# A decoder layer with 32 experts: a pool opened ahead of the output projection holds five more tiles, the operand of the dispatch comes in two tiles, and two orders of instructions change

## The chip, the cores and the metric

One core of a Trainium2 chip runs the whole kernel. The metric is device time in microseconds of one execution. In this text PE is TensorE, DVE is VectorE, ACT is ScalarE, POOL is GpSimd, and SP is the queue that issues the weight transfers; SBUF is the on-chip memory of 128 partitions, PSUM the accumulators of TensorE in banks of 512 float32 columns.

## The reference

One layer on 272 rows (256 tokens and 16 meta tokens), width 2048, all in float32. A mixer of two branches ends in an output projection; then comes a mixture of 32 experts, of which each token uses two:

```python
def mixer(x, ...):
    ...
    merged = (jax.nn.sigmoid(gm) * (y_m @ w_pm)
              + jax.nn.sigmoid(ga) * (y_a.reshape(B, L, A_W) @ w_pa))
    return merged @ w_out

def hier_moe(x2, w_group, b_group, w_router, b_router, w_gate_up, w_down):
    ...                                  # group, then two experts in it, per token
    def run_block(args):
        toks, ws, e = args
        xb = x2[toks]
        gu = xb @ w_gate_up[e]           # 2048 x 1024
        hb = jax.nn.silu(gu[:, :D_FF]) * gu[:, D_FF:]
        return ((hb @ w_down[e]) * ws[:, None]).astype(x2.dtype)   # 512 x 2048
    ...

h = layer_norm(ALPHA * h + mix, ln1_g, ln1_b)
h = layer_norm(ALPHA * h + hier_moe(h, ...), ln2_g, ln2_b)
```

The weights of the 32 experts are 32 x 12 MiB; they are read once.

## The kernel before

**Output projection.** `w_out` comes in 16 blocks of 1 MiB (`wo_r`, line 114, three buffers), four for each of four column blocks n. ACT and DVE split each block into a high and a low part, and PE multiplies with both (`wo_p`, line 285). Meanwhile PE also turns the residual `u` column by column into `uTb` and multiplies it with the router's weights (`plg`).

**Weight stream.** The expert weights come in chunks of 1 MiB. In this text "chunk e,k" is the k-th of the eight gate/up chunks of expert e (`weg`), each 256 of the 2048 rows; a down-projection chunk is `wed`, and the last two experts' down projection comes in pieces by columns (`wel`). The dictionary `specs` sets one order for all of them; `issue(n)` puts the next ones, up to n in all, into SP's queue in that order. Each takes the next buffer from the list `free`; `used` gives the buffer back when PE has multiplied with the chunk. The list holds four buffers `x0` to `x3`, four `y0` to `y3`, four `m0` to `m3` and later `u0`, `u1`, each 8 KiB a partition, whose former contents die at different times: `m` with the last column block of the output projection, `u` in the first dispatch. The chunks in `extra` have buffers of their own that take no later chunk: 0,7 lies in four pieces in the tiles of `yh` and `yl`, and 1,0 and 1,1 lie in the place of the accumulator `acc`. The scheduler decides where the transfers stand between others on SP.

**Dispatch.** For each four experts, `dispatch(q)` gathers their tokens' rows by matmuls with a 0/1 matrix `oh`: 8 banks of PSUM, each with two halves of 256 columns (k even, k odd), and in each half two matmuls with the high part `uh` of the rows and two with the low part `ul`. DVE reads the even half into `xe` (line 1050), ACT the odd half (line 1047). The first dispatch does two banks ahead, and the other six one by one between the first gate/up chunks; the later ones do all eight together.

**Experts.** They go in pairs p: PE multiplies 16 gate/up chunks (`gu`), ACT and DVE make `hb`, PE turns it to `hT`; between the gate/up chunks of pair p it does the down projection of pair p-1 (`py`). ACT and DVE scale the result and split it (`yh`, `yl`, lines 1277 and 1278), PE scatters it back to token rows (`pc`), and DVE adds it to `acc` (line 1265). The last pair's down projection goes in five pieces of columns (`LASTP`, three of 512 and two of 256); for them `finish` also takes the statistics of the final normalisation on DVE (line 1250) and a product on POOL.

Of the kernel before, what the change touches and what calls it, by code (L numbers as in the profile page):

```python
# [12 lines left out]
F32 = mybir.dt.float32  # L13
F32R = mybir.dt.float32r
# [9 lines left out]
P = 128  # L24
D = 2048
KD = D // P
# [22 lines left out]
def trunk(ctx, tc, x, meta, ln_emb_g, ln_emb_b, rel_bias, w_in, conv_w, conv_b, b_ig, b_fg,  # L49
# [796 lines left out]
    def in_parts(nm, src):  # L846
        ws = [pre.tile([P, 512], F32, name=f"{nm}{i}", tag=("yh", "yl")[i % 2], bufs=2)
              for i in range(4)]
        for i, w in enumerate(ws):
            nc.sync.dma_start(out=w, in_=src[:, i // 2, i % 2 * 512:i % 2 * 512 + 512])  # L850
        return lambda kk, h: ws[2 * kk + h]

    extra.update({("g", 0, 7): in_parts, ("g", 1, 0): lambda *a: in_acc(0, *a),
# [10 lines left out]
    uTb = big.tile([P, 8, S], F32, name="uTb", tag=YT[3])  # L864
# [35 lines left out]
    for n in range(4):  # L900
        sl = slice(n * 512, n * 512 + 512)
        pts = tchunks(w_out, KD, mh_, ml_, n * 512, f"wo{n}")
        issue((4, 8, 10, 10)[n])
        for b in range(2):
            uv = u[b][:, sl]
            nc.vector.scalar_tensor_tensor(uv, uv, ALPHA, pts[b], op0=ALU.mult, op1=ALU.add)
            nc.vector.bn_stats(ust[:, b, n], uv)
        if n < 3:
            bg.append(route_cols(n))
        else:  # L910
            drain()
            for _ in route_cols(n):
                pass
# [5 lines left out]
    issue(NSLOT + 3)  # L919
# [97 lines left out]
    def dispatch(q):  # L1017
# [8 lines left out]
        xe = me.tile([P, KD, 4 * C], F32, name=f"xe{q}", tag="xe", bufs=1)  # L1026
        ohf = oh.rearrange("p b e c -> p b (e c)")

        def bank(kc):
# [10 lines left out]
            for k in (2 * kc, 2 * kc + 1):  # L1040
                pv = pt[:, k % 2 * 256:k % 2 * 256 + 256]
                for i, part in enumerate((uh, ul)):
                    for b in R2:
                        mm(pv, lhsT=part[:, b, rows_of(k)], rhs=ohf[:, b],
                           start=i == 0 and b == 0, stop=i == 1 and b == 1)
                if k % 2:
                    nc.scalar.activation(xe[:, k], pv, AF.Identity, bias=gbp[:, 1, k:k + 1],  # L1047
                                         scale=gbp[:, 0, k:k + 1])
                else:
                    nc.vector.tensor_scalar(xe[:, k], pv, gbp[:, 0, k:k + 1],  # L1050
                                            gbp[:, 1, k:k + 1], op0=ALU.mult, op1=ALU.add)
# [5 lines left out]
    def slots_of(q, ohf):  # L1057
# [9 lines left out]
        ohT = me.tile([P, 2, S], F32R, name=f"ohT{q}", tag="ohT", bufs=1)  # L1067
# [52 lines left out]
    def up_chunk(e, kc, xe, pg_):  # L1120
# [4 lines left out]
        for kk in range(2):  # L1125
            k = kc * 2 + kk
            lt = xe[:, k, s0:s0 + C]
            mm(pg_[other], lhsT=lt, rhs=w(kk, 0), start=k == 0,
                             stop=k == KD - 1)
            mm(pg_[mine], lhsT=lt, rhs=w(kk, 1), start=k == 0,  # L1130
                             stop=k == KD - 1)
# [7 lines left out]
    def up_turn(p, hb):  # L1139
# [4 lines left out]
        hT = me.tile([P, 4, P], F32, name=f"hT{p}", tag="hT", bufs=1)  # L1144
# [14 lines left out]
    issue(NSLOT + 5)  # L1159
# [78 lines left out]
    def rows_split():  # L1238
        nonlocal gr
        h = pre.tile([P, 512], F32R, name="grh", tag="yh", bufs=2)  # L1240
        gr = me.tile([P, 512], F32R, name="gr", bufs=1)
# [42 lines left out]
    for p in range(NE // 2):  # L1284
# [4 lines left out]
        for n in range(16):  # L1289
# [19 lines left out]
            if n == 7:  # L1309
                hb = me.tile([P, 512], F32, name=f"hb{p}", tag="hb", bufs=1)  # L1310
# [24 lines left out]
    f12 = me.tile([P, 2, D], F32, name="fin12", tag="xe", bufs=1)  # L1335
    fin += [f12[:, 0], f12[:, 1]]
    final_scale()
    nm5 = me.tile([P, 2, 4, 32], F32, name="nm5", tag="hb", bufs=1)
    nc.vector.memset(nm5, 1.0)
    gated = gated_of(LAST, cur)  # L1340
    for c0, n in LASTP:
# [5 lines left out]
        gated(c0, n, py)()  # L1347
# [101 lines left out]
    nmT = me.tile([P, 2, P], F32R, name="nmT", tag="hT", bufs=1)  # L1449
# [43 lines left out]
```

## Time and profile before

| | before |
|---|---|
| time, median of 3 runs (lowest, highest) | 1781.91 us (1778.19, 1784.15) |
| the profiled execution's own time, its span | 1773.8 us, 1772.1 us |
| busy share of the span: PE, DVE, ACT, POOL | 93%, 40%, 26%, 7% |
| mean granted TensorE clock | 0.98 of 2.4 GHz |
| read from HBM, written | 533.53 MB, 2.11 MB |
| weight chunks `weg`, `wed`, issue to landing (median) | 19.9 us |

The busy share is an average over stages with different limits, and a matmul's end is modelled, so 93% doesn't say that PE bounds the kernel; which resource is full is read stage by stage. The time that a weight chunk takes from issue to landing includes its place behind others that were issued before it.

### The profile page before, as it was taken

How to read it: one execution, taken by the hardware profiler on the slowest of the kernel's cores; microseconds unless marked ns; L12 is line 12 of the kernel's file. 1: busy time of each engine (PE TensorE's matmuls, PEld its weight loads, DVE VectorE, ACT ScalarE, POOL GpSimd, SP SyncE). 2: the span in 40 equal slices, each digit the busy share in tenths (PEclk: the TensorE clock that was granted, in tenths of full speed). 3: DMA queues.
4: the chain of work that ended last, by engine and by line, in shares of the span. 5: the costliest groups of instructions: out<-in, count | busy, mean ns of one | idle time of the engine just before them, and what ended most of it. 6: DMA issues, size and time to landing. Idle time of an engine off the chain costs nothing. (4 is left out here: it accounts for less than half of the span.)

```text
span 1772.1 us, 20945 instructions
## 1 busy us (share of the span) xinstructions
PE 1648.9 (93%) x8488; PEld 1013.8 (57%) x8488; DVE 707.9 (40%) x1178; ACT 457.5 (26%) x695; POOL 118.2 (7%) x143
## 2 busy tenths in 40 slices
PE   8999999999999999989989899899897988988986
PEld 7988899988787787873343433432433334324332
DVE  7666754454646556452223323421212123202224
ACT  5343444444443443341110100110111001101111
POOL 3002000000302102000100000000000000000002
PEclk9999999999999999999999999999999999999998
DMA  7534454456565578648999999999999999999993
GB/s 221 169 108 132 144 167 143 143 190 229 179 204 178 167 260 301 222 165 303 418 419 420 419 420 419 420 420 419 420 419 419 419 420 420 419 420 419 420 409 118
DMA packets 155941, 537.06 MB, mean 303 GB/s; under 512 B 15724, under 2 KB 64076, under 8 KB 107824
## 3 DMA queue, kind: packets, MB, share of 16 engines
q1 hardware_dynamic: 153552, 530.54, 77.8%
q0 software_dynamic: 2224, 5.12, 1.0%
q8 instruction: 68, 1.11, 0.3%
q14 instruction: 33, 0.27, 0.0%
q10 hardware_dynamic: 64, 0.02, 0.0%
HBM read 533.53 MB, written 2.11 MB: 302 GB/s over the span
## 5 line engine op out<-in xcount | busy, mean ns | idle before, releaser
L1007 PE MATMUL gu<-weg,xe 128*64 128x512 f32 x2032 | 495.5, 610 | 30.5 <-DMA weg<-in_w_gate_up_dram 30.4
L1007 PEld LDWEIGHTS gu<-weg,xe 128*64 128x64 f32 x2032 | 140.2, 139 | 312.0 <-issue 246.9
L1007 PE MATMUL py<-wed,hT 128*64 128x512 f32 x960 | 246.4, 597 | 0.0
L1007 PEld LDWEIGHTS py<-wed,hT 128*64 128x64 f32 x960 | 69.6, 139 | 140.1 <-issue 138.7
L1277 ACT ACTIVATE yh<-py,gsl 128x512 fp32r<-128x512 f32 (+1 forms) x65 | 44.2, 681 | 355.3 <-PE py L1007 340.7
L1278 DVE SCALAR_TENSOR_TENSOR yl<-py,gsl,yh 128x512 fp32r<-128x512 f32 (+1 forms) x65 | 48.0, 738 | 194.4 <-ACT yh L1277 194.4
L1137 DVE TENSOR_TENSOR hb<-gu,hb 64x512 f32<-64x512 f32 x32 | 22.0, 689 | 243.7 <-ACT hb L1136 243.6
L1265 DVE TENSOR_TENSOR acc<-pc,acc 128x512 f32<-128x512 f32 (+1 forms) x122 | 78.9, 678 | 88.1 <-PE pc L1007 87.3
L1136 ACT ACTIVATE hb<-gu 64x512 f32<-64x512 f32 x32 | 18.9, 591 | 341.6 <-PE gu L1007 341.6
L1007 PE MATMUL pxe<-oh,uh 128*128 128x256 f32 x256 | 61.1, 321 | 46.1 <-DVE xe L1050 42.7
L1007 PEld LDWEIGHTS pxe<-oh,uh 128*128 128x128 f32 x256 | 40.9, 199 | 67.8 <-DVE xe L1050 55.8
L1251 POOL TENSOR_TENSOR fin<-acc,fin 128x512 f32<-128x512 f32 (+1 forms) x10 | 10.3, 1053 | 895.0 <-DVE acc L1265 895.0
L1050 DVE TENSOR_SCALAR xe<-pxe,gbp 128x256 f32<-128x256 f32 x64 | 34.7, 543 | 83.8 <-PE pxe L1007 83.8
L1007 PE MATMUL pc<-yh,ohT 128*128 128x512 f32 (+1 forms) x130 | 59.8, 460 | 6.0 <-ACT yh L1277 3.5
L1047 ACT ACTIVATE xe<-pxe,gbp 128x256 f32<-128x256 f32 x64 | 36.0, 563 | 101.1 <-PE pxe L1007 101.1
L1007 PEld LDWEIGHTS pc<-yh,ohT 128*128 128x128 f32 x130 | 24.7, 190 | 54.9 <-issue 23.8
L1007 PE MATMUL pc<-yl,ohT 128*128 128x512 f32 (+1 forms) x130 | 52.4, 403 | 1.1 <-DVE yl L1278 0.9
L1007 PE MATMUL pxe<-oh,ul 128*128 128x256 f32 x256 | 52.4, 287 | 0.0
L1068 DVE TENSOR_SCALAR ohT<-prk,slot 128x512 fp32r<-128x512 f32 x8 | 6.0, 751 | 93.7 <-PE prk L1007 93.7
L1007 PEld LDWEIGHTS pxe<-oh,ul 128*128 128x128 f32 x256 | 41.4, 201 | 0.0
L1007 PEld LDWEIGHTS pc<-yl,ohT 128*128 128x128 f32 x130 | 25.0, 193 | 4.6 <-DVE yl L1278 2.5
L760 POOL TENSOR_TENSOR gms<-gms,gas 128x512 f32<-128x512 f32 x8 | 10.9, 1389 | 224.0 <-DVE gas L759 224.0
(924 smaller groups left out, 3036.7 us busy)
## 6 DMA issues: line engine op xcount, KB each, us to landing
weg<-in_w_gate_up_dram SPq DMA_DIRECT2D x253, 1024.0 KB, 19.9
wed<-in_w_down_dram SPq DMA_DIRECT2D x120, 1024.0 KB, 19.9
gm_r<-in_w_in_dram SPq DMA_DIRECT2D x16, 1024.0 KB, 5.0
ga_r<-in_w_in_dram SPq DMA_DIRECT2D x16, 1024.0 KB, 5.1
wo_r<-in_w_out_dram SPq DMA_DIRECT2D x16, 1024.0 KB, 5.4
qk_r<-in_w_in_dram SPq DMA_DIRECT2D x8, 1024.0 KB, 5.7
mv_r<-in_w_in_dram SPq DMA_DIRECT2D x8, 1024.0 KB, 5.3
aq_r<-in_w_in_dram SPq DMA_DIRECT2D x8, 1024.0 KB, 5.2
```

Of the source, the lines that this page charges most:

```text
L760: nc.gpsimd.tensor_tensor(sg[0][:, b], sg[0][:, b], sg[1][:, b], op=ALU.add)
L1007: late(nc.tensor.matmul(*a, **k))
L1047: nc.scalar.activation(xe[:, k], pv, AF.Identity, bias=gbp[:, 1, k:k + 1], scale=gbp[:, 0, k:k + 1])
L1050: nc.vector.tensor_scalar(xe[:, k], pv, gbp[:, 0, k:k + 1], gbp[:, 1, k:k + 1], op0=ALU.mult, op1=ALU.add)
L1068: nc.vector.tensor_scalar(ohT.rearrange("p a b -> p (a b)"), pr, slot, None, op0=ALU.is_equal)
L1136: nc.scalar.activation(hb[mine], pg_[other], AF.Silu)
L1137: nc.vector.tensor_tensor(hb[mine], pg_[mine], hb[mine], op=ALU.mult)
L1251: nc.gpsimd.tensor_tensor(fin[1 + b][:, c0:c0 + n], acc[:, b, c0:c0 + n], fin[0][:, c0:c0 + n], op=ALU.mult)
L1265: nc.vector.tensor_tensor(av, pc[:, :n], av, op=ALU.add)
L1277: nc.scalar.activation(yh[:, :n], py[:, :n], AF.Copy, scale=gate)
L1278: nc.vector.scalar_tensor_tensor(yl[:, :n], py[:, :n], gate, yh[:, :n].bitcast(F32), op0=ALU.mult, op1=ALU.subtract)
```

## The change

It has four parts.

- Chunk 0,6 comes in four pieces into the places of `hb`, `hT`, `gr` and `ohT`, and these four tiles and the tile `xa` move from the pool `me`, opened behind the output projection, to the pool `pre`, opened ahead of it. `uTb` leaves the buffer `y3` and shares `xa`.
- `issue` is called with 12 in place of 10 in the third and fourth column block, and with one more in the two calls behind; so 1,2 and 1,3 are issued under the output projection (into `y2`, `y3`), 1,4 to 1,7 into `m0` to `m3`, and the first two `wed` into `u0`, `u1`.
- `xe` becomes two tiles of eight k each (`xa` in `pre`, `xb` in `me`); in `bank`, the matmuls of both halves come first and both reads after them.
- In the loop over the last pieces, the combination of a piece is written behind the matmuls of the next piece.

```diff
-    def in_parts(nm, src):
-        ws = [pre.tile([P, 512], F32, name=f"{nm}{i}", tag=("yh", "yl")[i % 2], bufs=2)
-              for i in range(4)]
+    def in_parts(tags, nm, src):
+        ws = [pre.tile([P, 512], F32, name=f"{nm}{i}", tag=t, bufs=4 // len(tags))
+              for i, t in enumerate(tags * (4 // len(tags)))]
...
-    extra.update({("g", 0, 7): in_parts, ("g", 1, 0): lambda *a: in_acc(0, *a),
+    extra.update({("g", 0, 6): lambda *a: in_parts(("hb", "hT", "gr", "ohT"), *a),
+                  ("g", 0, 7): lambda *a: in_parts(("yh", "yl"), *a), ("g", 1, 0): lambda *a: in_acc(0, *a),
                   ("g", 1, 1): lambda *a: in_acc(1, *a)})
...
-    uTb = big.tile([P, 8, S], F32, name="uTb", tag=YT[3])
+    uTb = pre.tile([P, 8, S], F32, name="uTb", tag="xa")
...
     for n in range(4):
         sl = slice(n * 512, n * 512 + 512)
         pts = tchunks(w_out, KD, mh_, ml_, n * 512, f"wo{n}")
-        issue((4, 8, 10, 10)[n])
+        issue((4, 8, 12, 12)[n])
...
-    issue(NSLOT + 3)
+    issue(NSLOT + 4)
     free += [(up, t) for t in UT]
...
-        xe = me.tile([P, KD, 4 * C], F32, name=f"xe{q}", tag="xe", bufs=1)
+        xe = [pool.tile([P, 8, 4 * C], F32, name=f"xe{q}{i}", tag=("xa", "xb")[i], bufs=1)
+              for i, pool in enumerate((pre, me))]
...
                     for b in R2:
                         mm(pv, lhsT=part[:, b, rows_of(k)], rhs=ohf[:, b],
                            start=i == 0 and b == 0, stop=i == 1 and b == 1)
+            for k in (2 * kc, 2 * kc + 1):
+                pv = pt[:, k % 2 * 256:k % 2 * 256 + 256]
                 if k % 2:
-                    nc.scalar.activation(xe[:, k], pv, AF.Identity, bias=gbp[:, 1, k:k + 1],
+                    nc.scalar.activation(xe[k // 8][:, k % 8], pv, AF.Identity, bias=gbp[:, 1, k:k + 1],
                                          scale=gbp[:, 0, k:k + 1])
                 else:
-                    nc.vector.tensor_scalar(xe[:, k], pv, gbp[:, 0, k:k + 1],
+                    nc.vector.tensor_scalar(xe[k // 8][:, k % 8], pv, gbp[:, 0, k:k + 1],
                                             gbp[:, 1, k:k + 1], op0=ALU.mult, op1=ALU.add)
...
-        ohT = me.tile([P, 2, S], F32R, name=f"ohT{q}", tag="ohT", bufs=1)
+        ohT = pre.tile([P, 2, S], F32R, name=f"ohT{q}", tag="ohT", bufs=1)
...
-            lt = xe[:, k, s0:s0 + C]
+            lt = xe[k // 8][:, k % 8, s0:s0 + C]
...
-        hT = me.tile([P, 4, P], F32, name=f"hT{p}", tag="hT", bufs=1)
+        hT = pre.tile([P, 4, P], F32, name=f"hT{p}", tag="hT", bufs=1)
...
-    issue(NSLOT + 5)
+    issue(NSLOT + 6)
...
-        gr = me.tile([P, 512], F32R, name="gr", bufs=1)
+        gr = pre.tile([P, 512], F32R, name="gr", bufs=1)
...
-                hb = me.tile([P, 512], F32, name=f"hb{p}", tag="hb", bufs=1)
+                hb = pre.tile([P, 512], F32, name=f"hb{p}", tag="hb", bufs=1)
...
-    f12 = me.tile([P, 2, D], F32, name="fin12", tag="xe", bufs=1)
-    fin += [f12[:, 0], f12[:, 1]]
+    fin += [pool.tile([P, D], F32, name=f"fin{i + 1}", tag=("xa", "xb")[i], bufs=1)
+            for i, pool in enumerate((pre, me))]
     final_scale()
-    nm5 = me.tile([P, 2, 4, 32], F32, name="nm5", tag="hb", bufs=1)
+    nm5 = pre.tile([P, 2, 4, 32], F32, name="nm5", tag="hb", bufs=1)
...
     gated = gated_of(LAST, cur)
+    then = None
     for c0, n in LASTP:
         py = pyp.tile([P, 512], F32, name=f"py{LAST}_{c0}", tag="py")
         for kk in range(4):
             for i in range(2):
                 mm(py[i * 64:i * 64 + 64, :n], lhsT=hTs[LAST][:, kk, 64 - i * 64:128 - i * 64],
                                  rhs=live["l", NE - 2 + i, c0][:, kk], start=kk == 0, stop=kk == 3)
-        gated(c0, n, py)()
+        nxt = gated(c0, n, py)
+        if then:
+            then()
+        then = nxt
+    then()
```

Where this puts the instructions, at three places. First SP's queue at the first dispatch: the transfers that are issued as PE uses up the first chunks (`weg_3` is chunk k = 3 of its expert, here experts 1 and 2; `wed_0`, `wed_1` are chunks of the down projection). Before:

```order
L823 DMA wed_0_7052<-in_w_down_dram 128x2048
L823 DMA weg_0_7069<-in_w_gate_up_dram 128x2048
L823 DMA weg_1_7088<-in_w_gate_up_dram 128x2048
L823 DMA weg_2_7105<-in_w_gate_up_dram 128x2048
L823 DMA weg_7_7027<-in_w_gate_up_dram 128x2048
L823 DMA wed_0_7029<-in_w_down_dram 128x2048
L823 DMA weg_3_7124<-in_w_gate_up_dram 128x2048
L823 DMA wed_1_7141<-in_w_down_dram 128x2048
L823 DMA wed_1_7147<-in_w_down_dram 128x2048
L823 DMA weg_4_7169<-in_w_gate_up_dram 128x2048
```

and with the change:

```order
L823 DMA weg_0_7061<-in_w_gate_up_dram 128x2048
L823 DMA weg_1_7078<-in_w_gate_up_dram 128x2048
L823 DMA weg_2_7097<-in_w_gate_up_dram 128x2048
L823 DMA weg_3_7114<-in_w_gate_up_dram 128x2048
L823 DMA wed_0_7036<-in_w_down_dram 128x2048
L823 DMA wed_0_7038<-in_w_down_dram 128x2048
L823 DMA wed_1_7133<-in_w_down_dram 128x2048
L823 DMA wed_1_7150<-in_w_down_dram 128x2048
L823 DMA weg_4_7176<-in_w_gate_up_dram 128x2048
```

Chunk 1,7 (`weg_7`) stood fifth among them and now stands ahead of the dispatch; nine rows stood ahead of `weg_4` (chunk 2,4), and now eight do.

Then PE in the second dispatch, where the eight banks lie together (`pxe_0`, `pxe_1`, `pxe_2` are banks; a wait is for the engine in brackets). Before:

```order
L1007 MATMUL pxe_0_7470<-oh_7466,uh 128x256 [waits DVE_49]
L1007 MATMUL pxe_0_7470<-oh_7466,uh 128x256
L1007 MATMUL pxe_0_7470<-oh_7466,ul 128x256 x2
L1007 MATMUL pxe_0_7470<-oh_7466,uh 128x256 [waits DVE_49]
L1007 MATMUL pxe_0_7470<-oh_7466,uh 128x256
L1007 MATMUL pxe_0_7470<-oh_7466,ul 128x256 x2
L1007 MATMUL pxe_1_7481<-oh_7466,uh 128x256 x2
L1007 MATMUL pxe_1_7481<-oh_7466,ul 128x256 x2
L1007 MATMUL pxe_1_7481<-oh_7466,uh 128x256 [waits DVE_49]
L1007 MATMUL pxe_1_7481<-oh_7466,uh 128x256
L1007 MATMUL pxe_1_7481<-oh_7466,ul 128x256 x2
L1007 MATMUL pxe_2_7492<-oh_7466,uh 128x256 [waits Activation_49]
```

and with the change:

```order
L1008 MATMUL pxe_0_7478<-oh_7473,uh 128x256 [waits DVE_49]
L1008 MATMUL pxe_0_7478<-oh_7473,uh 128x256
L1008 MATMUL pxe_0_7478<-oh_7473,ul 128x256 x2
L1008 MATMUL pxe_0_7478<-oh_7473,uh 128x256 x2
L1008 MATMUL pxe_0_7478<-oh_7473,ul 128x256 x2
L1008 MATMUL pxe_1_7489<-oh_7473,uh 128x256 [waits DVE_49]
L1008 MATMUL pxe_1_7489<-oh_7473,uh 128x256
L1008 MATMUL pxe_1_7489<-oh_7473,ul 128x256 x2
L1008 MATMUL pxe_1_7489<-oh_7473,uh 128x256 x2
L1008 MATMUL pxe_1_7489<-oh_7473,ul 128x256 x2
L1008 MATMUL pxe_2_7500<-oh_7473,uh 128x256 [waits Activation_49]
```

The matmuls are the same and stand in the same order; the wait for DVE in the middle of each bank is gone, and a bank's first matmul waits for DVE or, from the third on, for ACT. In the first dispatch it is the same, there with `gu` rows between the banks.

Last PE at the first two of the five last pieces (`py_0`, `py_512` are the products of the pieces, `pc_00` and `pc_01` the two halves of the scatter of the first). Before:

```order
L1007 MATMUL py_0_11275<-wel_0_11117,hT_11229 64x512
L1007 MATMUL pc_00_11288<-yh_0_11284,ohT_11142 128x512
L1007 MATMUL pc_00_11288<-yl_0_11285,ohT_11142 128x512
L1007 MATMUL pc_01_11295<-yh_0_11284,ohT_11142 128x512
L1007 MATMUL pc_01_11295<-yl_0_11285,ohT_11142 128x512
L1007 MATMUL py_512_11302<-wel_512_11119,hT_11229 64x512
L1007 MATMUL py_512_11302<-wel_512_11127,hT_11229 64x512
```

and with the change:

```order
L1008 MATMUL py_0_11290<-wel_0_11131,hT_11243 64x512
L1008 MATMUL py_512_11303<-wel_512_11133,hT_11243 64x512
L1008 MATMUL py_512_11303<-wel_512_11141,hT_11243 64x512
L1008 MATMUL py_512_11303<-wel_512_11133,hT_11243 64x512
L1008 MATMUL py_512_11303<-wel_512_11141,hT_11243 64x512
L1008 MATMUL py_512_11303<-wel_512_11133,hT_11243 64x512
L1008 MATMUL py_512_11303<-wel_512_11141,hT_11243 64x512
L1008 MATMUL py_512_11303<-wel_512_11133,hT_11243 64x512
L1008 MATMUL py_512_11303<-wel_512_11141,hT_11243 64x512
L1008 MATMUL pc_00_11316<-yh_0_11299,ohT_11156 128x512
L1008 MATMUL pc_00_11316<-yl_0_11300,ohT_11156 128x512
L1008 MATMUL pc_01_11323<-yh_0_11299,ohT_11156 128x512
```

The scatter of a piece moved behind all eight matmuls of the next piece; on DVE the statistics and the additions of one piece now stand between the scaling and the additions of the next.

## Rows read from the trace of the kernel before

**Rows 1.** The page, part 2: the span in 40 equal slices of 44.3 us; busy share of PE in tenths (9 is 90% or more), and GB/s that the DMA engines moved. The seventeenth to the twentieth digit and number are 709 to 886 us.

```profile
PE   8999999999999999989989899899897988988986
GB/s 221 169 108 132 144 167 143 143 190 229 179 204 178 167 260 301 222 165 303 418 419 420 419 420 419 420 420 419 420 419 419 419 420 420 419 420 419 420 409 118
```

**Rows 2.** Busy time of each engine in two stretches of 10 us around the first dispatch: stretch, its length, then busy us and instructions of PE, PEld, DVE, ACT, POOL; the last three columns are the granted TensorE clock as a share of full speed, the DMA engines' busy share, and GB/s.

```profile
790.00:800.00 10.00, 8.05 (x25) 4.61 (x26) 2.99 (x6) 7.01 (x15) 0.00 (x0) 0.52 0.00 0
830.00:840.00 10.00, 10.00 (x48) 3.19 (x46) 0.60 (x2) 0.59 (x1) 0.00 (x0) 1.00 0.87 322
```

**Rows 3.** Timeline of the SP queue from 799 to 836 us (start, time from the first issue to the last one's end, line, buffer and tensor, how many in a row).

```profile
799.95 0.33 SPq L823 DMA_DIRECT2D wed<-in_w_down_dram  x1
803.88 10.19 SPq L823 DMA_DIRECT2D weg<-in_w_gate_up_dram  x4
814.35 0.33 SPq L823 DMA_DIRECT2D wed<-in_w_down_dram  x1
815.71 0.33 SPq L823 DMA_DIRECT2D weg<-in_w_gate_up_dram  x1
819.66 4.27 SPq L823 DMA_DIRECT2D wed<-in_w_down_dram  x2
830.47 5.48 SPq L823 DMA_DIRECT2D weg<-in_w_gate_up_dram  x4
```

**Rows 4.** Timeline of PE from 790 to 839 us: start, us, operation, output and operands, how many, and in brackets the idle time before it and what ended it. `pxe` is the dispatch, `gu` the experts' gate/up product.

```profile
790.60 0.80 PE L1007 MATMUL pxe<-oh,uh 128*128 128x256 f32 x2 [1.19 <-ACT u L948]
792.54 0.80 PE L1007 MATMUL pxe<-oh,uh 128*128 128x256 f32 x2 [0.71 <-DVE xe L1050]
793.13 0.63 PE L1007 MATMUL pxe<-oh,ul 128*128 128x256 f32 x2
793.56 0.63 PE L1007 MATMUL pxe<-oh,uh 128*128 128x256 f32 x2
...
796.40 3.50 PE L1007 MATMUL gu<-weg,xe 128*64 128x512 f32 x8
799.84 0.52 PE L1007 MATMUL pxe<-oh,uh 128*128 128x256 f32 x2
800.19 0.40 PE L1007 MATMUL pxe<-oh,ul 128*128 128x256 f32 x2
801.23 0.51 PE L1007 MATMUL pxe<-oh,uh 128*128 128x256 f32 x2 [0.64 <-DVE xe L1050]
...
801.91 1.94 PE L1007 MATMUL gu<-weg,xe 128*64 128x512 f32 x8
803.77 0.52 PE L1007 MATMUL pxe<-oh,uh 128*128 128x256 f32 x2
...
828.54 10.47 PE L1007 MATMUL gu<-weg,xe 128*64 128x512 f32 x48
```

**Rows 5.** Timeline of PE, 1690 to 1720 us: the only two rows there that waited for a weight transfer.

```profile
1694.77 3.68 PE L1007 MATMUL gu<-weg,xe 128*64 128x512 f32 x8 [4.44 <-DMA weg<-in_w_gate_up_dram]
...
1709.73 1.94 PE L1007 MATMUL gu<-weg,xe 128*64 128x512 f32 x8 [0.51 <-DMA weg<-in_w_gate_up_dram]
```

**Rows 6.** Timeline rows of one `w_out` block: its issue on the SP queue, and the first instruction that reads it (ACT).

```profile
727.03 0.37 SPq L114 DMA_DIRECT2D wo_r<-in_w_out_dram  x1
...
738.77 1.05 ACT L122 CAST wo_20h<-wo_r 128x1024 fp32r<-128x1024 f32 x1 [1.48 <-PE wo_p L285]
```

**Rows 7.** The page, part 6: DMA issues of one kind: buffer and tensor, queue, how many, KB each, median us from issue to landing.

```profile
wo_r<-in_w_out_dram SPq DMA_DIRECT2D x16, 1024.0 KB, 5.4
```

**Rows 8.** Chain of waits of PE over the whole span: what waited, for what, us in total, how often, longest.

```profile
PE pxe L1007 <- DVE xe L1050: 42.7, 64, 1.0
```

**Rows 9.** Timeline rows of dispatches: the DVE and the ACT instruction that read the two halves of one bank of the first dispatch (800 us), then four PE rows from the middle of the third (1003 us).

```profile
800.63 0.54 DVE L1050 TENSOR_SCALAR xe<-pxe,gbp 128x256 f32<-128x256 f32 x1 [4.23 <-PE pxe L1007]
...
802.02 0.56 ACT L1047 ACTIVATE xe<-pxe,gbp 128x256 f32<-128x256 f32 x1 [2.86 <-PE pxe L1007]
...
1002.76 0.51 PE L1007 MATMUL pxe<-oh,uh 128*128 128x256 f32 x2 [0.91 <-DVE xe L1050]
...
1003.35 0.40 PE L1007 MATMUL pxe<-oh,uh 128*128 128x256 f32 x2
1003.59 0.40 PE L1007 MATMUL pxe<-oh,ul 128*128 128x256 f32 x2
1004.63 0.51 PE L1007 MATMUL pxe<-oh,uh 128*128 128x256 f32 x2 [0.64 <-DVE xe L1050]
```

**Rows 10.** Timeline of all engines from 1729 us on, rows of the first of the five last pieces, and the last DVE row before the final normalisation.

```profile
1729.90 3.65 PE L1007 MATMUL py<-wel,hT 128*64 128x512 f32 x16
...
1734.32 0.75 DVE L1278 SCALAR_TENSOR_TENSOR yl<-py,gsl,yh 128x512 fp32r<-128x512 f32 x1 [5.26 <-ACT yh L1277]
...
1734.34 0.49 PE L1007 MATMUL pc<-yh,ohT 128*128 128x512 f32 x1 [0.79 <-ACT yh L1277]
...
1735.66 1.29 DVE L1265 TENSOR_TENSOR acc<-pc,acc 128x512 f32<-128x512 f32 x2 [0.59 <-PE pc L1007]
...
1736.02 3.65 PE L1007 MATMUL py<-wel,hT 128*64 128x512 f32 x16
...
1736.87 1.40 DVE L1250 BATCH_NORM_STATS2 st<-acc 128x6 f32<-128x256 f32 x4
...
1756.02 0.74 DVE L1250 BATCH_NORM_STATS2 st<-acc 128x6 f32<-128x256 f32 x2
```

More of the change, by code (lines that the diff above doesn't have):

```diff
@@ L1448, in trunk @@
         nc.tensor.transpose(pn5[:, b], nm5[:, b].rearrange("p a b -> p (a b)"), ident)
-    nmT = me.tile([P, 2, P], F32R, name="nmT", tag="hT", bufs=1)
+    nmT = pre.tile([P, 2, P], F32R, name="nmT", tag="hT", bufs=1)
     nc.vector.tensor_copy(nmT, pn5)
```

## The prediction, made before the changed kernel had run

> **What bounds the kernel now.** I read the 40 slices first, to see which resource is full in which stretch. From the twentieth slice (842 us) to the third last, DMA moves 418 to 420 GB/s without a dip; the three from 709 to 842 us move 222, 165 and 303 [rows 1]. So the expert weights bound the second half, and the first half is bound by something else. Then the windows, for where the change-over lies: 790 to 800 us moves nothing, 830 to 840 us 322 GB/s [rows 2]. Then the SP queue, which issues the weights in its order, each when its buffer is free: nine chunks at 799.95 to 823.6 us, a pause, and from 830.47 us on four in 5.5 us [rows 3]. The pause is PE's doing: a chunk's buffer comes free when PE has multiplied it, and the three chunks after the seventh (0,7; 1,0; 1,1) lie in buffers that take no later chunk, so nothing is issued until chunk 1,2 has been used, in the stream that ends with 48 `gu` rows at 828.54 us [rows 4]. From there a chunk costs PE about 1.7 us (10.47 us for 48 rows of eight a chunk) against 1.05 MB / 420 GB/s = 2.5 us on the DMA engines, so the queue never empties again. Hence three stretches: PE's pace up to the 25th issue (830.47 us); then the DMA engines alone; and, after the last gate/up chunks (PE last waits for one at 1709.73 us [rows 5]), a chain of PE, ACT and DVE. What brings the 25th issue forward brings forward all weights after it by as much. A wait on PE in between is worth nothing.
>
> **More chunks under the output projection.** Sixteen chunks are now in SP's queue before the dispatch instead of fifteen, two of them between the `w_out` blocks. I cost this at nothing, for and against. For: the order on SP shows that the 25th chunk still waits for the use of 1,2. Before, 15 ahead and 9 until the pause make 24; after, 16 and 8 (0,6 now lies in pieces and frees no buffer) make 24 too. The DMA engines have emptied their queue by then, so a chunk loaded earlier only lengthens the pause. Against: the two chunks take 5.0 us of DMA in slices that move 165 to 222 GB/s. A `w_out` block is issued 11.7 us before its first use (727.03 to 738.77 us [rows 6]) and lands 5.4 us after its issue [rows 7]: 6.3 us of cover, 3.8 behind a chunk. If that cover were gone, each block would cost PE what it comes late. The pieces of 0,6 wait for what the pieces of 0,7 waited for before. The smaller tiles (`hb`, `hT`, `gr`, `ohT`) are written only after 0,6 has been used, and `uTb`'s place is read for the last time before `xe` needs it: nothing.
>
> **Halves of a bank.** In all 64 banks of the dispatches PE stops between the halves until DVE has read the first, 42.7 us in all [rows 8], most often 0.64 us, as at 801.23 [rows 4]. Only the first dispatch lies before the 25th issue, so only its eight banks count.
> Two banks ahead of the first `gu`, at the lower clock: now 790.60 to 796.40 = 5.80 us. Without a stop, sixteen matmuls go at the pace of the rows at 792.54, 793.13 and 793.56: one pair 0.59, seven 0.43, and 0.12 to switch: 3.72. That saves 2.1.
> Six banks between `gu` chunks, full clock: now 799.84 to 801.91 = 2.07 each. Without a stop: 0.35 (799.84 to 800.19), three pairs of 0.24 (1003.35 to 1003.59 [rows 9]), 0.09 to switch: 1.16. That saves 0.91 each, 5.5.
> The granted clock is 1.2 GHz from about 790 to 799.6 us (mean 0.52 [rows 2]; `gu` takes 3.50 at 796.40 and 1.94 at 801.91); before it fell PE had been idle, waiting for the routing, and before it rose it had run a `gu` chunk of 3.50 us without a stop. If it rises at the same moment, the third bank now falls into that stretch and takes 2.0 instead of 1.16: minus 0.8. If it rises sooner because PE now runs without stops from 790.60, that 0.8 is not lost, and the first `gu` (3.50 against 1.94 at full clock) gets up to 1.6 back. I take the same moment, the case the rows show: 2.1 + 5.5 - 0.8 = **6.8 us**; ends 6 (each bank 0.1 late for another reason) and 9 (the clock). The 25th issue comes at about 823.7 us. Are the 24 through by then? By the same savings the last five are issued from about 808 to 814 us and need 12.5 us: done about 822, just in time. That caps any further gain at some 2 us.
> The reads now both follow the second half. In the order after, ACT's read waits for DVE's, so a bank is free 0.54 + 0.56 us [rows 9] and three hand-overs of about 0.1 after its last matmul, 2.5 us after its first. In the first dispatch that is covered: a `gu` chunk of 1.9 us lies between banks, and two banks are used in turn. In the later ones two banks in turn give 1.25 us a bank against 1.87 now (1002.76 to 1004.63): 5 us less PE time a dispatch, under DMA, worth nothing.
> The Trainium skill ("PSUM — Partial Sum Buffer", PSUM bank collisions raise a hardware error) has a rule that speaks against this part: no two engines may access one bank at once, not even to read it, and waits go by the bank, not by the columns. The rows agree (PE waits for DVE though it writes other columns); two reads at once are shown by no row. By the rule a later bank costs 1.25 us, without it PE's own 1.07; the sum is the same by both.
>
> **The last pieces.** Now a piece of 512 columns takes 6.12 us (1729.90 to 1736.02): 3.45 of matmuls, then PE waits for `yh` and `yl`, then 1.2 for the four `pc` matmuls (1734.34 to 1736.02 less 0.46 of waiting for `yl`) [rows 10]. After, PE runs the next piece's `py` during `yh` and `yl`. I lay it out from the start of the first piece: `py` at 0, 3.45 and 8.2; `pc` of the pieces at 7.0, 11.7, 14.7. From the third on DVE is late: per piece it has 0.75 (`yl`), 1.29 (`acc`) and 1.40 (statistics) [rows 10], with about 2.0 for each piece of 256 columns 14.3 us over the five, in an order that mixes two pieces, and PE's second `pc` half waits for a bank that DVE reads late (15.4). Then `py` of the last piece 16.0 to 17.75, its `yl` 18.75 to 19.25, its `acc` to 22.15, its statistics to 22.9. Before, they end at 1756.02 + 0.74 - 1729.90 = 26.9. Gain **4.0 us**; ends 2 (each mixed DVE step 0.5 late) and 5.9 (PE alone). The weights are there: the last slice (from 1728 us) moves 118 GB/s, 5.2 MB [rows 1], 2.1 of them the output, so 3.1 MB of weights remain, 8 us at 2.5 us a chunk, through at about 6; the last are needed at 16.0.
>
> **Sum.** The profiled execution took 1773.8 us (span 1772.1): 1773.8 - 6.8 - 4.0 = 1763.0. The median of the runs shown, 1781.9, is 8.1 above it; the terms are differences, so I take them off the median too: **1771.1 us**, -0.6%. About 0.3% (5.3 us) is what a measurement can tell from no change.
>
> **Rivals.**
> (a) *A slow clock at the end.* Later dispatches are 5 us shorter, so PE reaches the DMA engines' pace earlier and stands longer at the two down-projection chunks between groups of four. After such a wait of 4.44 us the next chunk took 3.68 instead of 1.94 us [rows 5], and the group lost about 2.5 us. Now this falls on the last group but one; the last waited only 0.51. If it falls on the last, its 2.5 us reach the end: 1773.6. 20%. The Trainium skill ("TensorE: Matmul & The Clock Gate", HAM oscillation — how this bites in real kernels) tells the same of a kernel whose PE waits for DMA between groups; the row agrees.
> (b) *The clock rises sooner* in the first dispatch: 9 instead of 6.8: 1768.9. For it: no stops any more; against: the rows show only one such rise. 13%.
> (c) *Preloading pays by itself*: the 25th chunk is not held by 1,2, and two chunks of 2.5 us come on top: 1766.1. Against it the count of 24 on both sides. 5%.
> (d) *The chunks do little*: the end pieces gain nothing because DVE's mixed order delays them, and (a) holds: 6.8 - 2.5 = 4.3, 1777.6, no change that can be told. 12%.
> (e) *Slower*: `w_out` starves. SP issues in order, and the pieces of 0,6 stand ahead of a `w_out` block. With 6.3 us of cover it decides when a block is held over 6.3 + 10.8 = 17 us; a hold of 23 us would give 1771.1 + 23 - 6.3 = 1787.8. Against it: PE is 90% busy or more in the slice from 709 us and 80% in the next [rows 1], with the pieces of 0,7 waiting in the same queue for the same tiles. 5%.
> My own case has the rest, 45%.
>
> **How the numbers follow.** Faster by over 0.3% are my case, (a), (b), (c): 83%. Within it (d): 12%. Slower (e): 5%. The range goes from a little below (c) to (d), 1764.5 to 1778: it leaves out (e) and the outer parts of (c) and (d), and takes in 6 to 9 for the first term and 2 to 5.9 for the second. Within my own case alone it is 1768 to 1774.
>
> **What would show it.** The seven-microsecond term: no PE wait for DVE inside a bank, first `gu` at about 794.3 us, the 25th weight issue near 823.7 us, DMA full from about 826 us. If that issue stays at 830, or moves without the last `gu` group moving with it, the term is wrong. Preloading: the windows from 720 to 760 us move more, PE stays full there, and the pause before the 25th issue stays. The end: first `py` to last statistics 22.9 us instead of 26.9, DVE without gaps at its close. Rival (a) shows as a lower granted clock in the last 20 us before the first of the last pieces; (e) as PE idle before 780 us.

## The result, and the profile after

The changed kernel takes 1765.55 us (median of 5 runs, 1763.74 to 1770.84), the kernel before beside it 1781.91 (1778.19 to 1784.15): ratio 0.9916, 95% interval 0.9894 to 0.9938, or 15 us less (11 to 19); by the two medians it is 16.4. Forecast were 1771.1 us, 10.8 less, with a range from 1764.5 to 1778. The profiled execution of the changed kernel took 1768.8 us, span 1767.1. That is only 5.0 us under the profiled execution of before, so the first question is what those two executions differ in beside the change.

Page, part 2, and two windows of the changed kernel, to set beside [rows 1, 2]; then the windows with the pause in front of the 25th weight chunk (columns as in [rows 2]):

```profile
PE   8999999999999999999999898998988989989986
GB/s 209 174 104 145 144 145 159 151 168 237 169 212 172 191 215 276 319 167 282 417 419 420 419 420 419 419 419 420 419 420 419 420 419 419 420 420 419 419 410 138
...
790.00:800.00 10.00, 7.96 (x45) 7.26 (x46) 7.56 (x35) 9.55 (x16) 2.50 (x2) 0.67 0.08 33
830.00:840.00 10.00, 10.00 (x49) 3.37 (x46) 3.04 (x21) 1.18 (x2) 0.97 (x2) 1.00 1.00 414
...
824.00:826.00 2.00, 2.00 (x12) 0.60 (x10) 0.10 (x1) 0.00 (x0) 0.00 (x0) 1.00 0.94 393
826.00:828.00 2.00, 2.00 (x12) 0.70 (x10) 0.00 (x0) 0.00 (x0) 0.00 (x0) 1.00 0.00 0
```

The seventeenth slice (from 707 us here) moves 319 GB/s instead of 222 (the preloaded chunks), and PE shows no gap there. The second half moves 417 to 420 as before. DMA is again empty just ahead of the 25th issue (826 to 828 us).

SP's queue in the changed kernel, to set beside [rows 3], and PE from the first dispatch on, beside [rows 4]:

```profile
802.87 9.41 SPq L823 DMA_DIRECT2D weg<-in_w_gate_up_dram  x4
814.40 3.93 SPq L823 DMA_DIRECT2D wed<-in_w_down_dram  x4
827.91 5.48 SPq L823 DMA_DIRECT2D weg<-in_w_gate_up_dram  x4
```

```profile
784.02 1.07 PE L285 MATMUL wo_p<-wo_31l,mTh 128*128 128x512 f32 x4
...
787.75 2.04 PE L879 MATMUL plg<-wg,uTb 128*128 128x40 f32 x12
789.59 5.04 PE L130 MATMUL warm<-ident 128*128 128x128 f32 x22
...
797.06 0.64 PE L1008 MATMUL pxe<-oh,uh 128*128 128x256 f32 x2 [1.16 <-DVE oh L1023]
...
798.81 0.63 PE L1008 MATMUL pxe<-oh,uh 128*128 128x256 f32 x2
...
799.80 3.03 PE L1008 MATMUL gu<-weg,xe 128*64 128x512 f32 x8
802.76 0.52 PE L1008 MATMUL pxe<-oh,uh 128*128 128x256 f32 x2
803.11 0.40 PE L1008 MATMUL pxe<-oh,ul 128*128 128x256 f32 x2
803.35 0.40 PE L1008 MATMUL pxe<-oh,uh 128*128 128x256 f32 x2
803.59 0.40 PE L1008 MATMUL pxe<-oh,ul 128*128 128x256 f32 x2
803.92 1.94 PE L1008 MATMUL gu<-weg,xe 128*64 128x512 f32 x8
```

Eight rows stand ahead of the 25th issue, which comes at 827.91. Between `gu` chunks a bank takes 1.16 us (802.76 to 803.92), the forecast's figure. But the last `w_out` matmuls start at 784.02 here and at 778.90 in the profile of before: the profiled executions are 5.1 us apart before the first dispatch begins. Windows from long before that, where the change alters nothing, show a part of how (columns as above, the third last is the granted clock). First before, with its PE rows behind the `w_out` matmuls (`warm` are matmuls that only keep PE busy during the routing):

```profile
778.90 1.07 PE L285 MATMUL wo_p<-wo_31l,mTh 128*128 128x512 f32 x4
...
782.70 1.43 PE L878 MATMUL plg<-wg,uTb 128*128 128x40 f32 x12
783.96 2.70 PE L130 MATMUL warm<-ident 128*128 128x128 f32 x22
...
100.00:110.00 10.00, 10.00 (x73) 8.87 (x73) 6.40 (x17) 4.58 (x8) 0.54 (x2) 1.00 0.63 204
550.00:560.00 10.00, 8.98 (x43) 7.17 (x42) 8.19 (x12) 3.52 (x7) 1.58 (x3) 0.98 0.71 231
```

and the changed kernel:

```profile
100.00:110.00 10.00, 10.00 (x64) 8.72 (x64) 6.49 (x17) 3.77 (x7) 0.54 (x2) 0.88 0.46 135
550.00:560.00 10.00, 8.98 (x26) 6.85 (x27) 8.83 (x12) 3.12 (x6) 4.40 (x4) 0.52 0.59 166
```

The waits of PE, to set beside [rows 8], two of its waits for weights, beside [rows 5], and the last pieces, beside [rows 10]:

```profile
PE gu L1008 <- DMA weg<-in_w_gate_up_dram: 59.3, 25, 5.5
PE pxe L1008 <- ACT xe L1051: 6.3, 21, 0.8
```

```profile
1692.31 3.13 PE L1008 MATMUL gu<-weg,xe 128*64 128x512 f32 x8 [4.46 <-DMA weg<-in_w_gate_up_dram]
1707.27 1.94 PE L1008 MATMUL gu<-weg,xe 128*64 128x512 f32 x8 [1.73 <-DMA weg<-in_w_gate_up_dram]
...
1727.70 8.44 PE L1008 MATMUL py<-wel,hT 128*64 128x512 f32 x32
1736.07 0.50 PE L1008 MATMUL pc<-yh,ohT 128*128 128x512 f32 x1
1737.20 3.65 PE L1008 MATMUL py<-wel,hT 128*64 128x512 f32 x16
...
1749.82 0.74 DVE L1269 TENSOR_TENSOR acc<-pc,acc 128x256 f32<-128x256 f32 x2
1750.48 0.74 DVE L1254 BATCH_NORM_STATS2 st<-acc 128x6 f32<-128x256 f32 x2
```

No bank waits for DVE in its middle any more: 42.7 us became 6.3, for ACT and between banks. PE's waits for weights grew from 30.4 us to 59.3. The first two pieces' `py` now stand together, in 8.44 us, and DVE works without a gap at its close.

### The profile page after: what moved, and what is told of

It is laid out like the page before. It is cut to its first block, busy times and chain, and to the rows that moved or that the text cites. A ratio compares the mean times of both kernels' runs of the same rounds, so it can differ in the third digit from the quotient of the medians.

```text
span 1767.1 us, 20882 instructions
## 1 busy us (share of the span) xinstructions
PE 1653.9 (94%) x8488; PEld 1018.9 (58%) x8488; DVE 709.4 (40%) x1178; ACT 457.5 (26%) x695; POOL 118.1 (7%) x143
## 5 line engine op out<-in xcount | busy, mean ns | idle before, releaser
L1008 PE MATMUL gu<-weg,xe 128*64 128x512 f32 x2032 | 500.0, 615 | 59.3 <-DMA weg<-in_w_gate_up_dram 59.3
L1008 PE MATMUL py<-wed,hT 128*64 128x512 f32 x960 | 250.4, 606 | 0.0
L1008 PE MATMUL pxe<-oh,uh 128*128 128x256 f32 x256 | 55.8, 299 | 9.7 <-ACT xe L1051 6.3
L760 POOL TENSOR_TENSOR gms<-gms,gas 128x512 f32<-128x512 f32 x8 | 11.0, 1390 | 226.4 <-DVE gas L759 226.4
```

Source lines behind the costliest of these rows:

```text
L760: nc.gpsimd.tensor_tensor(sg[0][:, b], sg[0][:, b], sg[1][:, b], op=ALU.add)
L1008: late(nc.tensor.matmul(*a, **k))
```

## Experiments

Five landmarks make the traces comparable. In the table: start of the last `w_out` row; from there to the 25th weight issue; from there to the first `py` of the last pieces; from there to the end of the last statistics row; the rest; the span. All us, from one trace each; runs with one name are the same kernel on another chip. Gains in us are taken below from the measured ratio and its interval; some expectations take the difference of the medians instead, which is 10.3 for the halves, 9.0 for the last pieces and 13.6 for both.

| kernel | w_out | to 25th | to `py` | to statistics | rest | span |
|---|---|---|---|---|---|---|
| before | 778.9 | 51.6 | 899.4 | 26.9 | 15.3 | 1772.1 |
| before, again | 783.1 | 52.7 | 900.4 | 28.6 | 15.4 | 1780.2 |
| halves | 784.0 | 44.0 | 900.1 | 29.8 | 16.4 | 1774.2 |
| halves, first dispatch | 782.1 | 43.9 | 903.1 | 28.3 | 15.4 | 1772.8 |
| the same, again | 784.5 | 44.0 | 907.0 | 29.7 | 15.5 | 1780.7 |
| halves, later dispatches | 781.5 | 52.8 | 899.2 | 26.9 | 16.4 | 1776.7 |
| last pieces | 783.6 | 52.5 | 899.5 | 23.9 | 15.4 | 1774.9 |
| last pieces, again | 781.9 | 52.5 | 899.4 | 22.2 | 15.3 | 1771.3 |
| preloading | 782.5 | 52.6 | 899.7 | 28.6 | 16.1 | 1779.5 |
| halves and last pieces | 784.4 | 44.0 | 899.7 | 23.6 | 16.2 | 1767.9 |
| changed | 784.0 | 43.9 | 899.8 | 23.5 | 15.9 | 1767.1 |
| changed, again | 781.4 | 43.9 | 899.1 | 23.8 | 15.9 | 1764.1 |
| changed, 40 to keep warm | 779.8 | 41.6 | 899.4 | 22.2 | 16.2 | 1759.3 |
| the same, again | 779.1 | 41.6 | 899.3 | 22.2 | 16.0 | 1758.2 |

**Halves of a bank alone.**

```
                            start=i == 0 and b == 0, stop=i == 1 and b == 1)
+            for k in (2 * kc, 2 * kc + 1):
+                pv = pt[:, k % 2 * 256:k % 2 * 256 + 256]
                 if k % 2:
```

> The kernel before with one edit alone: in each bank of the dispatch both halves are multiplied before either is read; same tiles, same preloading, old order of the last pieces. Theory A (the sum on record): 6.8 us less than before, ends 6 and 9, so a ratio near 0.996; the 25th weight issue comes as much earlier, and the last group's waits for DMA by the same amount. Rival C (preloading pays by itself, and it is what carried the 16.4 us of the whole change past the 10.8 of the sum): also about 6.8 us here, and the rest in the run with preloading alone. Rival H (the halves give more in ordinary executions than the profiled one showed, since the granted clock falls in other places there): 10 us or more here, ratio 0.994 or less.

Measured: 0.9936 (0.9921 to 0.9951), 11.4 us less (8.7 to 14.1). 8.7 us of it stand ahead of the 25th issue (44.0 for 52.7). Other traces repeat that: five with the old order and the clock of ordinary executions take 52.5 to 52.8 us there, the six with the new order and 22 `warm` matmuls 43.9 to 44.0.

**The last pieces alone**, on two chips: the last hunk of the diff, nothing else.

> The kernel before with one edit alone: a last piece's combine runs after the next piece's py matmuls. Theory A: 4.0 us less than before (ends 2 and 5.9), ratio 0.9978, all of it between the first py of the last pieces and the last statistics (26.9 before, 22.9 by the sum; 23.5 measured in the whole change). Rival T (the tail carries the excess of the whole change): 8 us or more, ratio 0.9955 or less.

> The order of the last pieces alone, once more on another chip: the first time gave 9.0 us, while its own trace shows 5.0 against an ordinary execution of before (28.6 to 23.6 us from the first of the last py to the last statistics). Theory A with what the traces show: 5 us, ratio 0.997. Rival T: 9 us again, ratio 0.995, so that something outside the last 40 us gains 4 us by it.

Measured: 0.9943 (0.9925 to 0.9960), then 0.9975 (0.9959 to 0.9991): 10.2 and 4.5 us. The traces show 4.7 from the first `py` to the last statistics, whether the first `py` ran partly at the lower clock or not (28.6 to 23.9; 26.9 to 22.2). The second run agrees with them; what gave the first its other 5 us (4 by the medians) no trace shows.

**Preloading alone**: the change without the two reorderings.

> The changed kernel without the two reorderings: sixteen chunks instead of fifteen queued ahead of the dispatch, two of them between the w_out blocks, the moved tiles and the split xe tile, but the halves and the last pieces in the old order. Theory A: nothing that can be told, within 2 us of before, ratio 0.999 to 1.001, with the 25th weight issue as long after the end of the w_out matmuls as before (51.6 us) and a longer pause ahead of it. Rival C (preloading pays by itself): 5 us less, ratio 0.997. Rival E (w_out blocks come late): slower than before.

Measured: 0.9989 (0.9977 to 1.0), 2.0 us (0 to 4.1), and 52.6 us to the 25th issue: nothing there, as costed. Rival (c) of the forecast falls.

**Both reorderings, no preloading.**

> The kernel before with both reorderings and without the preloading: the whole change less its part on pools and chunks. Theory A: the same gain as the whole change, 10.8 us by the sum and 16.4 by the medians already measured. If it gives 10.8 while the whole change gives 16.4, the preloading carries some 5 us, either by itself (rival C) or only once the halves have shortened PE's time ahead of the 25th chunk, so that without it the queue is not through in time (rival I): then the DMA engines show no pause ahead of the 25th issue here, and the chunks ahead of it land late.

Measured: 0.9917 (0.9901 to 0.9934), 14.8 us: the whole gain without the preloading. The two parts apart gave 11.4 and 4.5 to 10.2.

**The kernel before, once more.**

> The kernel before, unchanged, for a second profiled execution: the one on record took 1773.8 us, below each of the 17 timed executions (1779.2 to 1786.9), and four variants all end their w_out matmuls at 782.5 to 784.4 us where it ended them at 778.9. Theory L (the profiled execution was a lucky one, its granted clock stood at 2.4 GHz in stretches where it usually falls): here the w_out matmuls end at 782 to 785 us, the 25th weight issue comes 52.5 us later as in the variants with the old halves (51.6 in the first profile), the first of the last py takes 5 to 6.6 us instead of 3.65, and the whole takes 1780 to 1785. Rival O (an ordinary execution loses its 8 us in one place that the variants do not show, since two edits apart gave 10.3 and 9.0 us and together 13.6): one of the stretches between these landmarks is 5 us longer than in every variant.

Measured: 1780.65 us, ratio 1.0 (0.9980 to 1.0019), profiled at 1781.9. Rows of this trace, PE and DVE:

```profile
783.13 1.07 PE L285 MATMUL wo_p<-wo_31l,mTh 128*128 128x512 f32 x4
...
796.04 0.82 PE L1007 MATMUL pxe<-oh,uh 128*128 128x256 f32 x2 [1.16 <-DVE oh L1022]
...
801.87 3.40 PE L1007 MATMUL gu<-weg,xe 128*64 128x512 f32 x8
...
807.27 1.94 PE L1007 MATMUL gu<-weg,xe 128*64 128x512 f32 x8
...
1736.28 5.35 PE L1007 MATMUL py<-wel,hT 128*64 128x512 f32 x16
...
1764.11 0.74 DVE L1250 BATCH_NORM_STATS2 st<-acc 128x6 f32<-128x256 f32 x2
```

Theory L holds: against the first profile of before 4.2 us are lost ahead of the last `w_out` row, 1.1 up to the 25th issue, 1.0 in the stream and 1.7 in the last pieces (the first `py` takes 5.35 us, not 3.65). Before rounding, these are the 8.1 us between the two profiles. The first was a lucky one. For the last pieces and the stretch up to the dispatch the rows show that it is the clock (22 `warm` matmuls take 2.70 us in the first profile, 3.95 here). For the 4.2 us the two windows shown above bear it out in part (0.91 and 0.83 in this trace, 1.00 and 0.98 in the first); for the 1.0 us in the stream it is not shown.

**Halves in the first dispatch alone**, on two chips, and **in the later ones alone** (the same edit with `q > 0`). `fill` multiplies a half, `read` reads it.

```
+            jobs = [(f, k) for k in (2 * kc, 2 * kc + 1) for f in (fill, read)]
+            if q == 0:
+                jobs = [jobs[i] for i in (0, 2, 1, 3)]
+            for f, k in jobs:
+                f(k, pt[:, k % 2 * 256:k % 2 * 256 + 256])
```

> The kernel before with the halves reordered in the eight banks of the first dispatch alone; the 56 later banks as before. Theory A: the same gain as with all 64 banks (10.3 us by the medians of that run), since later dispatches lie under the DMA stream: ratio 0.993 to 0.996, and the span from the end of the w_out matmuls to the 25th weight issue is 44 us instead of 52.5. Rival S (all waits count): an eighth of that gain, 1.3 us.

> The kernel before with the halves reordered in the first dispatch alone, once more, for a second trace. The first gave 4.8 us where all 64 banks gave 10.3, and its trace shows one later dispatch (1478 to 1499 us) in which the granted clock fell to 1.2 GHz between the stops, then a stretch from 1500 to 1516 us in which DMA moved 290 to 390 GB/s. Theory D (the stops in a bank are no harm to PE's time under DMA, but they let the clock fall in some executions, PE then comes too late for the buffers, and the DMA stream loses some 3 us): here too at least one later dispatch runs below 0.7 of the full clock when the execution takes 1774 us or more, and none does when it takes 1771 or less. Rival X (chance of that one chip): no such dispatch, time 1770 to 1774.

> The kernel before with the halves reordered in the 56 banks of the later dispatches alone. Theory A: nothing, within 2 us of before, although PE loses 37 us of waiting for DVE; its waits for DMA grow by as much. Rival (a) of the prediction (later dispatches that are shorter bring a slow clock into the last group of chunks): 2.5 us slower. Rival S (all waits count): 9 us faster.

Measured: first dispatch alone 0.9973 (0.9955 to 0.9991) and 0.9964 (0.9941 to 0.9986), 4.8 and 6.4 us; later ones alone 0.9998 (0.9982 to 1.0014), 0.4 us. The later ones alone do what Theory A says, nothing; the first alone gives neither the whole gain of Theory A nor the 1.3 us of rival S. The first part wins its 8.7 us ahead of the 25th issue (43.9 and 44.0) and loses some of them in the DMA stream: 903.1 and 907.0 us where it takes 899 to 900 in the others. Windows of the second trace over the third dispatch, PE rows from it, and SP's next weights:

```profile
1000.00:1004.00 4.00, 2.42 (x15) 2.02 (x16) 2.18 (x4) 0.78 (x2) 0.00 (x0) 1.00 1.02 422
...
1012.00:1016.00 4.00, 3.36 (x15) 2.93 (x14) 0.55 (x1) 1.13 (x2) 0.00 (x0) 0.50 1.01 416
...
1028.00:1032.00 4.00, 4.00 (x18) 1.45 (x16) 1.93 (x4) 0.00 (x0) 0.00 (x0) 1.00 0.58 223
1032.00:1036.00 4.00, 4.00 (x20) 1.35 (x20) 1.13 (x2) 0.00 (x0) 0.00 (x0) 1.00 0.75 272
...
1001.69 0.52 PE L1007 MATMUL pxe<-oh,uh 128*128 128x256 f32 x2 [0.90 <-DVE xe L1051]
1003.56 0.51 PE L1007 MATMUL pxe<-oh,uh 128*128 128x256 f32 x2 [0.64 <-DVE xe L1051]
1014.08 0.79 PE L1007 MATMUL pxe<-oh,uh 128*128 128x256 f32 x2 [0.64 <-DVE xe L1051]
1016.79 0.80 PE L1007 MATMUL pxe<-oh,uh 128*128 128x256 f32 x2 [0.64 <-DVE xe L1051]
...
1005.92 2.82 SPq L823 DMA_DIRECT2D wed<-in_w_down_dram  x2
1025.82 11.26 SPq L823 DMA_DIRECT2D weg<-in_w_gate_up_dram  x4
```

At 1003.56 the stops of 0.64 us still stand at 2.4 GHz (a bank takes 1.87 us); then the clock falls to 1.2 GHz and a bank takes 2.71 (1014.08 to 1016.79). The first weights after the dispatch are issued at 1025.82 us, 17 us after the last ones were, and DMA runs at 223 and 272 GB/s; in the second trace of before the gap at the same dispatch is 9.8 us, and DMA stays at 414 GB/s or more up to 1030 us. The same fall comes from 1370 to 1390 us, and once in the first trace, from 1482 to 1502: against the 899.5 us of the others the stream loses about 3.5 us with one such dispatch and 7.5 with two. The eight executions stand in two groups: 1767.7 to 1771.9 us, mean granted clock 0.977 to 0.979, and 1778.9 to 1782.5 us, 0.965 to 0.967; the traced one, 1782.5, is of the second. Theory D holds for both traces. That the group at 1768 has no such dispatch no trace shows. So the later banks are worth nothing alone, and some 5 to 7 us once the start has been won (11.4 for all, 4.8 and 6.4 for the first alone, each on another chip). As far as the traces go it takes both, the early start and the stops: the clock falls in 3 of the 14 later dispatches of these two, in none of 35 in the five traces with the old order throughout ([rows 9] is from one), and in none of 49 in the seven with the new order in the later dispatches. Why it stays up among the same stops after a late start is open.

**Forty matmuls to keep PE busy in the routing, instead of 22**, on two chips, the second with the changed kernel beside it:

```
-    keep_warm(11, "warm1")
+    keep_warm(20, "warm1")
```

> The changed kernel with 40 instead of 22 matmuls that keep PE busy during the routing, ahead of the first dispatch. In the profiles the granted clock falls there: the 22 take 5.04 us (2.70 at 2.4 GHz), the first two banks 2.74 and the first gu chunk 3.03 (1.94 at 2.4 GHz). Theory K (PE's idle time during the routing is what lets the clock fall): the 40 take 4.9 us, the first two banks and the first gu run at 2.4 GHz, 2.7 us less in all. Rival N (the clock falls before these matmuls, in the transposes and logits ahead of them, and stays down): the 40 take 9.2 us, end after the routing is done and hold the first dispatch by 3.3 us: slower by 3.3 less what the clock gives back behind them.

> The changed kernel, on the same chip as the two others. By the traces 8.8 us (start) and 5.0 (last pieces) less than before: 13.8, ratio 0.992; the medians on record differ by 16.4.

> The changed kernel with 40 instead of 22 matmuls that keep PE busy during the routing, on the same chip as the changed kernel itself. Its first trace shows 41.6 us from the end of the w_out matmuls to the 25th weight issue instead of 43.9. Theory K: 2.3 us faster than the changed kernel, ratio to before 0.9905 to 0.991. Rival N: no difference that can be told, since the clock falls ahead of these matmuls in other executions, and the 40 then hold the dispatch.

Measured: 0.9916 (0.9892 to 0.9940) on the first chip. On the second 0.9891 (0.9872 to 0.9911), median 1760.27, for the changed kernel 0.9928 (0.9910 to 0.9947), median 1767.69. Rows of the second trace:

```profile
782.81 1.43 PE L879 MATMUL plg<-wg,uTb 128*128 128x40 f32 x12
784.07 4.71 PE L130 MATMUL warm<-ident 128*128 128x128 f32 x40
...
792.94 1.08 PE L1008 MATMUL gu<-weg,xe 128*64 128x512 f32 x4
...
1720.02 7.09 PE L1008 MATMUL py<-wel,hT 128*64 128x512 f32 x32
...
1741.48 0.74 DVE L1254 BATCH_NORM_STATS2 st<-acc 128x6 f32<-128x256 f32 x2
```

In both traces the forty run at 2.4 GHz, 4.71 us where 22 took 5.04, and the 25th issue comes 2.2 us sooner; in the second the two banks ahead of the first `gu` take 2.24 us (790.70 to 792.94), 2.80 in the changed kernel beside it (794.38 to 797.18). But not all of the 2.2 us is the work of the forty. In both traces PE reaches them at 2.4 GHz: the twelve `plg` matmuls just ahead take 1.43 us, as in the first profile of before, against 2.04 and 2.12 in the two traces of the changed kernel, and the edit leaves those matmuls alone. In that profile of before 22 took 2.70, and its first bank starts 11.7 us after the last `w_out` row; with forty it is 11.6, in the two traces of the changed kernel 13.0. So about 1.4 us come with the clock that PE arrives with. The other 0.8 fit Theory K: behind the 22 of that profile PE stood idle for 2.37 us and the clock fell to 1.2 GHz, behind the forty it stood idle for 0.38 and the clock stayed at 2.4. What the forty do when the clock has fallen ahead of them (rival N) no trace shows. The other 3.7 us between the two spans (1764.1, 1758.2) lie where this edit does not reach: 2.3 ahead of it, and 1.6 in the last pieces, less 0.2 in the stream. The last pieces gain it because their `py` runs at 2.4 GHz here, as it also does in the second run of the last pieces alone. On the second chip all five executions of this version (1759.9 to 1762.1) are below all six of the changed kernel (1764.1 to 1770.4); how much of that is the edit, and how much the clock that PE arrives with, stays open.

## Why the prediction was right, and where its sizes were off

**What bounds the kernel**: right. From the 25th issue to the first of the last `py` it takes 899 to 900 us in twelve of fourteen traces, whatever was edited ahead of it.

**Preloading at nothing**: right. 24 chunks stand ahead of the 25th on both sides, the pause is still there (826 to 828 us), and alone it gives 0 to 4.1 us. `w_out` did not starve (rival (e)): PE has no gap from 720 to 760 us.

**Halves, 6.8 us**: right mechanism, too small. Against an ordinary execution of before it is 8.8 (52.7 to 43.9). The six banks between `gu` chunks gave 5.5, as forecast. The two ahead of the first `gu` gave 3.1, not 2.1 (5.83 from 796.04 to 801.87, now 2.74 from 797.06 to 799.80): the forecast put all sixteen matmuls at the lower clock, and in this trace ten of them ran at 2.4 GHz, up to 798.5 us, before the clock fell. The 0.8 for a third bank at 1.2 GHz failed outright: it ran at 2.4 GHz, and the first `gu` took 3.03 us instead of 3.40, a gain of 0.4. That is rival (b), at half its price. This goes with the order of the halves, as far as twelve traces tell: the first `gu` takes 2.96 to 3.04 us in the six traces with the new order there (and 22 to keep warm) and 3.21 to 3.50 in the six with the old.

**Later banks at nothing**: the step that failed, "What brings the 25th issue forward brings forward all weights after it by as much. A wait on PE in between is worth nothing." The bank's time was right: two banks take 2.48 us (998.50 to 1000.98), 1.24 each, and each pair waits 0.28 for ACT.

```profile
998.50 0.52 PE L1008 MATMUL pxe<-oh,uh 128*128 128x256 f32 x2 [0.32 <-DVE acc L1269]
...
1000.98 0.52 PE L1008 MATMUL pxe<-oh,uh 128*128 128x256 f32 x2 [0.28 <-ACT xe L1051]
```

The forecast's estimate was 1.25 by the rule of the Trainium skill that it weighed, "PSUM — Partial Sum Buffer" (PSUM bank collisions raise a hardware error), that no two engines may access a bank at once; this trace agrees. The price of the bank was not right. It was taken from a profile in which the later dispatches hold 2.4 GHz; with the start won and the stops left in, some of them fall to 1.2 GHz in both traces, and of the 8.7 us that the 25th issue came forward the stream loses about 3.5 and 7.5. The sum did not have to pay for this only because the change takes the stops out of the later dispatches as well, which the forecast counted for nothing: that part of the total is luck.

**Last pieces, 4.0 us**: 4.7 by the traces at full clock (26.9 to 22.2; 22.9 was forecast), 5.1 with the slower first `py` (28.6 to 23.5). The layout charged DVE with too much delay: in the second trace with forty the last `yl` starts at 18.4 us after the first `py`, not 18.75, and the last `acc` ends at 21.5, not 22.15.

**Rival (a)** did not come by its mechanism: the last group's wait is 1.73 us with the `gu` after it at 1.94, and the chunk that is slow, 3.13 us, belongs to the last group but one, as before. Its sign, a lower clock ahead of the first of the last pieces, shows at the very end of those 20 us (0.63 from 1726 to 1730 us); but it shows in the unchanged kernel too (0.84 and 0.74 from 1734 to 1742 us in its second trace), so the change is not needed for it.

**The sum**: 8.8 + 5.1 = 13.9 us, measured 15.0 (11 to 19) and, on another chip, 12.8 (9.4 to 16.0). The forecast's 10.8 is 3.1 too small. Some 1.4 of that come of sizing on one execution that ran 8.1 us under the median, with the clock falling at other places than in ordinary ones: 1.0 at the two banks ahead of the first `gu`, 0.4 at the first `py`. The rest are terms mis-sized for other reasons: 1.2 at the third bank and the first `gu`, where the clock rose sooner, and 0.7 in the layout of the last pieces, less some 0.2 lost elsewhere ahead of the 25th issue. Taking the sum off the median was right; taking the sizes from the lucky trace was not.

## What to carry to other kernels

Where a stream of transfers is the bound, look for the instruction that its first held-up issue waits for, and shorten only what lies ahead of it; then ask whether the shorter kernel still keeps its pace behind it. If the profiled execution lies outside the timed ones, compare several traces by landmarks before a term is sized on one. Short stops in PE's row are not free under DMA when they can cost the clock. Before an edit is credited with a faster clock, see whether the rows ahead of it ran at that clock already.

## What was not expected of the hardware

In the third dispatch of the second trace with halves in the first dispatch alone the granted clock fell from 2.4 to 1.2 GHz after stops of 0.31, 0.90 and 0.64 us, with no longer wait in the 20 us before. The Trainium skill ("TensorE: Matmul & The Clock Gate", HAM oscillation — how this bites in real kernels) tells of the fall behind waits of several us for DMA. The row at 1692 us agrees with it: behind a wait of 4.46 us the chunk takes 3.13 instead of 1.94. This dispatch is another case, without such a wait. And where the clock falls differs from execution to execution in parts that were not edited: the last `w_out` row starts anywhere from 778.9 to 784.5 us.
